# A hybrid decoder layer on one core: x requested at once over two queues, and B's keys and values as plain 512-column products behind the first products on h

## The chip, the core and the metric

The kernel runs on one core of a Trainium2 chip. The metric is the time of one execution in device microseconds; three runs of the kernel before took 1562.09, 1558.93 and 1561.91 us. The core's engines work side by side, each through its own instructions in order: TensorE (PE) multiplies, VectorE (DVE), ScalarE (ACT) and GpSimd (POOL) do the rest, SyncE (SP) mostly starts transfers. ScalarE and GpSimd can start transfers too, and every engine that does has a queue of its own for them.

## The reference

One layer on x (512 rows of 2048 numbers) with a memory of 256 rows. One projection of h = RMSNorm(x) feeds three attention branches:

```python
h = rmsnorm(x, norm_g[l])
(a_q, a_ckv, i_q, i_k, i_w, a_gate,
 b_q, b_k, b_v, b_gate,
 c_q, c_gate, mix_gate) = split_cols(h @ w_in[l], IN_SIZES)
ckv = rmsnorm(a_ckv, kv_norm_g[l])
a_k, a_v = jnp.split(ckv @ w_kv_up[l], 2, axis=-1)
...
kb = rmsnorm(b_k.reshape(bsz, seq, B_KV_HEADS, B_HEAD_DIM), k_norm_b[l])
vb = b_v.reshape(bsz, seq, B_KV_HEADS, B_HEAD_DIM)
...
m_k, m_v = jnp.split(rmsnorm(mem, mem_norm_g[l]) @ w_mem_kv[l], 2, axis=-1)
...
merged = g_a * (oa @ w_up_a[l]) + g_b * (ob @ w_up_b[l]) + g_c * (oc @ w_up_c[l])
x = x + merged @ w_o[l]
```

A attends to the 128 keys per row that an indexer (i_q, i_k, i_w) picks, B to a window of 128 rows with two key and value heads of 64 each, C to the memory. `b_k` and `b_v`, the subject here, are together 256 columns of the projection.

## The kernel before, in words

All arrays lie transposed: 128 channels on the partitions, the 512 rows of x along the free axis. A product in float32 is made of three in a shorter form: every operand is split into a high and a low part, and high x high, low x high and high x low are added up (`mm3`, L294 to L296). The high part of a weight is a cast on ScalarE (L276, `wh`), the low part a subtraction on VectorE (L278, `wl`), each for half a unit of 128 x 1024 weights (`split`).

Every half unit is one step of a fixed order. `next_hb` (L287) opens step i: it splits the half unit four steps ahead (`LA`), and then does what `plan` has put down for step i: start a transfer, square a tile of x, sum it, norm it. So the place of an instruction in its engine's queue comes from the step numbers. Raw weights have three buffers (`raw`), `wh` and `wl` six each.

The stages up to the point that matters are these.

- Memory units: 12 of the 16 units of the memory's keys and values (`mem`, L460), 6 products `mm3` of 512 columns in two half steps per unit and accumulator group. Beside them x is loaded (L368, on ScalarE's queue, three steps ahead of its use), squared (L374) and summed up (L377). The rows' mean (L379) and the inverse root (L306, GpSimd) give h through `x_norm`, `x_high` and `x_low`.
- g1 (L473): 192 products of 336 columns on h: the indexer's key and weights, and the latent a_ckv.
- The last four memory units (L589). Beside them two generators run, a step of each at every `pump()`: `g_lat` norms, scales and transposes the latent (L499 to L519), `g_comb` (L552) makes from h the sums and differences that the pairs below need, and overwrites half of h's high and low parts with one of them.
- KV (L691): the latent times `w_kv_up`, three groups of 24 products; `kv_group` (L655) squares, norms, transposes (L681) and stores keys and values. It has three buffers `sq`, some of which are held until a store (L667, L687) has landed.
- Pairs (`pair`, L780): all other projections of h go by two at a time, as a scheme of 7 products of half size (256 columns, 8 x 3 each) in the place of 8. Sums of weight tiles for it are made by GpSimd (L212) and by transfers that add (L218). `STREAM` (L96) is the order of the pairs: first B's keys and values (`bkv`), then a pair of the merge gates (`mix`), four pairs of the indexer's queries (`iq`), and so on. `kv_b` (L1040) norms and transposes B's keys after their pair.

From the indexer pairs on nothing is changed.

Of the kernel before, what the change touches and what calls it, by code (L numbers as in the profile page):

```python
# [45 lines left out]

LG = {"c0": 1, "c1": 2, "c2": 3, "c3": 1, "a0": 3, "a1": 1, "a2": 3, "a3": 3, "b0": 2, "b1": 1, "b2": 2, "b3": 2, "b4": 2, "kb0": 6, "kb1": 4, "kb2": 2, "kb3": 3, "kv0": 1, "kv1": 2, "kv2": 1, "kv3": 1, "m0": 6, "m1": 4, "m2": 3, "m3": 4, "m4": 7, "m5": 3, "l0": 2, "l1": 2, "l2": 2, "l3": 2, "iq": 1, "limit": 3, "gapc": 5, "gapa": 6, "gapb": 6, "cb0": 1, "cb1": 1, "ol": 3, "s1": 9, "s2": 5, "s3": 5, "s4": 2, "nq0a": 3, "nq1a": 1, "pta": 1, "nq0b": 3, "nq1b": 1, "ptb": 1, "nq0c": 3, "nq1c": 1, "ptc": 1}


class Pump:
# [43 lines left out]
def _stream():  # L96

    mix = [("mix", j, d) for d in range(0, KT, 2) for j in range(3)]
    s = [("bkv",), mix.pop(0)] + [("iq", j) for j in range(4)] + [mix.pop(0)]
    for name, n in (("c", HC), ("a", HA), ("b", 6)):  # L100
        for h in range(n):
            s += [(name, h), mix.pop(0)]
        if name != "b":
            s.append(mix.pop(0))
    return s + mix


STREAM = _stream()


@with_exitstack
def hybrid_layer(ctx: ExitStack, tc: tile.TileContext, xT, memT, memR, w_g1, w_un, w_up, params, consts, rel1, onehot, out):
# [139 lines left out]
    un = [w_un[k] for k in range(w_un.shape[0])]  # L252
    singles("mem", un[:K1])
    singles("g1", [w_g1[k] for k in range(8)])
    singles("mem2", un[K1:16])
    singles("kv", un[16:19])
    n_h = 19 + 4 * len(STREAM)
    pairs("h", un[19:n_h], POS["kv", 0] + 2)
    singles("upc", un[n_h:n_h + 8])
    singles("upa", [w_up[k] for k in range(16)])  # L260
    singles("upb", [w_up[k] for k in range(16, 32)])
# [102 lines left out]
            hx_new(k, F32)  # L364
        return hxf[k % 8][:, 2 * (k // 8):2 * (k // 8) + 2, :]

    def x_dma(k):
        act.dma_start(xf(k), xT[k].rearrange("p (a b) -> p a b", a=2))  # L368

    sqs = {}  # L370

# [47 lines left out]

    KO = [k + 8 * j for k in range(8) for j in range(2)]  # L420
    for k in range(KT):
        plan(k - 3, lambda k=k: x_dma(k))
        plan(k, lambda k=k: x_sq(k))
        if k:
            plan(k + 1, lambda k=k: x_sum(k))
    plan(KT + 1, rms_sum)
    plan(KT + 2, rms_pow)
    plan(KT + 4, rms_rows)
# [4 lines left out]
        plan(i_g1 - 3 + n, lambda k=k: x_norm(k))  # L433
    for c in range(8):
        i = POS["mem", 2 * c] if 2 * c < K1 else POS["mem2", 2 * c - K1]
        plan(i - 8, lambda c=c: m_dma(c))
        plan(i - 3, lambda c=c: m_split(c))


# [5 lines left out]
    dve.memset(gk, 0.0)  # L445
    act.activation(gk, gk, AF.Exp)
    sync.dma_start(pc, params)
    for f in at.pop(-8):
        f()
    tiles_["mem", 0] = wp.tile([128, 1024], F32, tag="raw", bufs=3, name=nm("wraw"))  # L450
    for c in (0, 512):
        sync.dma_start(tiles_["mem", 0][:, c:c + 512], un[0][:, c:c + 512])
    for i in range(-8, 0):
        step(i)
    plan(2, lambda: sync.dma_start(cc, consts))


# [94 lines left out]
    def g_comb():  # L552

        F = {}

        def sums(k):
            F[k] = f = cb.tile([128, 4, 256], F32, tag="tf", bufs=2, name=nm("tf"))
            b11, b12, b21, b22 = (xf(k + 8 * j)[:, c, :] for j in range(2) for c in range(2))
            dve.tensor_tensor(out=f[:, 3, :], in0=b11, in1=b12, op=ALU.subtract)
            dve.tensor_tensor(out=f[:, 0, :], in0=b22, in1=f[:, 3, :], op=ALU.add)  # L560
            dve.tensor_tensor(out=f[:, 1, :], in0=b12, in1=b22, op=ALU.subtract)
            dve.tensor_tensor(out=f[:, 2, :], in0=b21, in1=f[:, 0, :], op=ALU.subtract)

        def high(k):
            act.copy(hth[:, k, 256:], F[k][:, 3, :])
            hx_new(k, F32R)
            act.copy(hxt[k][:, 0:3, :], F[k][:, 0:3, :])

        def low(k):
            f = F.pop(k)  # L570
            dve.tensor_tensor(out=htl[:, k, 256:], in0=f[:, 3, :], in1=hth[:, k, 256:].bitcast(F32), op=ALU.subtract)
            dve.tensor_tensor(out=hxt[k][:, 3:6, :], in0=f[:, 0:3, :], in1=hxt[k][:, 0:3, :].bitcast(F32), op=ALU.subtract)

        for k in range(10):
            if 0 <= k - 2:
# [12 lines left out]


    mem(range(K1, KT))  # L590
# [578 lines left out]
        return tl("t2")  # L1169

    last = max(i for i, x in enumerate(STREAM) if x[0] == "b") + 3
    for n, item in enumerate(STREAM):
        kind = item[0]
        if n == last:
            flush()
            pump.drain()
            ws["stack"].close()
            ws.clear()
            switch("fp", {"t2": 4, "og": 1, "m": 2, "f": 1, "oxh": 1, "oxl": 1})
            oxh, oxl = tl("oxh", (128, 6, T), F32R), tl("oxl", (128, 6, T), F32R)  # L1180
            ox = [(oxh[:, k, :], oxl[:, k, :]) for k in range(6)]
            pump.back(o_load("c", ox[:4]))
        if item[0] not in ("mix", "iq") and item[-1] in ("bkv", 0):
            flush()
        if item == ("iq", 0):
            flush()
            pump.drain()
            ck_s.close()
            switch("iq", {"t2": 4, "stk": 6, "rl": 2, "mr": 2})
            pump.back(g_mem())  # L1190
            pump.back(g_index())
            pump.back(g_ik())
            pump.back(g_rel())
        elif item == ("c", 0):
            switch("c", {**BASE, "q": 2})
        elif item == ("a", 0):
            pump.drain()
            ws["stack"].close()
            cs_s.close()
            ws.clear()  # L1200
            pump.gap = LG["gapa"]
            switch("a", {**BASE, "q": 2, "T": 2, "kv": 2})
        elif item == ("b", 0):
            pump.drain()
            ws["stack"].close()
            tk_s.close()
            ws.clear()
            switch("b", {**BASE, "q": 4, "T": 2, "kb1": 1, "kb2": 1, "vb": 1})
            pump.gap = LG["gapb"]
            pump.back(b_start())  # L1210
        if kind == "bkv":
            pair(t2, t2, kv_b)
        elif kind == "iq":
            def fin(z0, z1, item=item):
                st = [stack(z, "stk") for z in (z0, z1)]

                def ready():
                    yield from lag("iq")
                    for x in range(2):
                        j = 2 * item[1] + x  # L1220
                        iq[2 * j], iq[2 * j + 1] = st[x]
                pump.back(ready())
            pair(t2, t2, fin)
        elif kind == "mix":
            def mix_fin(z0, z1, item):
                yield
                _, j, d = item
                for x, z in enumerate((z0, z1)):
# [168 lines left out]
def _layout(x, mem, norm_g, w_in, kv_norm_g, w_kv_up, idx_k_ln_g, idx_k_ln_b, q_norm_a, k_norm_a, q_norm_b, k_norm_b,  # L1397
# [13 lines left out]
    def pairs(a, b):  # L1411
# [64 lines left out]
```

## Time and profile before

| | us |
|---|---|
| runs, median of 3 | 1561.91 |
| the profiled execution | 1568.9 |
| its span | 1567.1 |
| TensorE busy | 1494.5 (95%) |
| VectorE busy | 1211.7 (77%) |
| ScalarE busy | 792.7 (51%) |
| GpSimd busy | 587.6 (37%) |
| TensorE's waits in the first 200 us, eight longest kinds | 30.4 |

The span is the profiled execution without what lies around it. Matmuls are pipelined: the time of one row of a matmul reaches into the next, so a sequence is best read from the starts of its rows. "Idle before" names what an engine had waited for when an instruction began.

### The profile page before, as it was taken

The numbers are of one execution on the slowest core, as the hardware profiler recorded it, in microseconds if no ns is written. First come the engines' busy times: TensorE is split into PE (matmuls) and PEld (weight loads), VectorE is DVE, ScalarE is ACT, GpSimd is POOL, SyncE is SP. The second block draws the span as 40 slices with busy tenths as digits, with TensorE's granted clock in tenths as the row PEclk, the third lists the DMA queues.
The fourth block names the chain that finished last, engine by engine and source line by source line (L and its number), as shares of the span: only waits on it lengthen the run. The fifth ranks groups of instructions, "written<-read, shape, count | busy, mean of one in ns | idle before, by whom it ended". The sixth has DMA issues, their size and how long they took to land. (4 is left out here: it accounts for less than half of the span.)

```text
span 1567.1 us, 29464 instructions
## 1 busy us (share of the span) xinstructions
PE 1494.5 (95%) x11066; PEld 1420.0 (91%) x11066; DVE 1211.7 (77%) x2020; ACT 792.7 (51%) x1673; POOL 587.6 (37%) x485
## 2 busy tenths in 40 slices
PE   7978998999999999999999999999989999989998
PEld 5867997989999999999999999999979888879998
DVE  5897678899997688778777778778856576996565
ACT  5555466655555455555555555555535332444342
POOL 0013442343333344333333434333323034865543
PEclk9889999999999999999999999999999999999999
DMA  8346578445446666556556555555546765547774
GB/s 300 119 124 170 160 193 218 118 128 166 122 144 180 174 183 183 178 135 189 179 156 170 160 136 165 173 128 168 156 132 180 248 205 169 180 124 196 201 196 129
DMA packets 98792, 263.75 MB, mean 168 GB/s; under 512 B 10356, under 2 KB 23796, under 8 KB 98650
## 3 DMA queue, kind: packets, MB, share of 16 engines
q1 hardware_dynamic: 78746, 197.77, 36.4%
q0 software_dynamic: 15264, 55.58, 20.0%
q10 hardware_dynamic: 4640, 8.52, 1.8%
q8 instruction: 87, 1.43, 0.4%
q14 instruction: 55, 0.45, 0.1%
HBM read 237.12 MB, written 29.04 MB: 170 GB/s over the span
## 5 line engine op out<-in xcount | busy, mean ns | idle before, releaser
L294 PE MATMUL p<-hth,wh 128*128 128x256 f32 (+1 forms) x1792 | 532.4, 297 | 12.0 <-ACT hth L1276 5.4
L295 PE MATMUL p<-htl,wh 128*128 128x256 f32 (+1 forms) x1792 | 521.7, 291 | 2.3 <-DVE htl L1278 2.3
L296 PE MATMUL p<-hth,wl 128*128 128x256 f32 (+1 forms) x1792 | 522.1, 291 | 1.4 <-DVE wl L278 1.3
L294 PE MATMUL p<-hx,wh 128*128 128x256 f32 x1272 | 371.0, 292 | 0.8 <-DVE t L763 0.8
L294 PEld LDWEIGHTS p<-hth,wh 128*128 128x128 f32 x1792 | 347.6, 194 | 22.5 <-ACT hth L1276 5.6
L296 PE MATMUL p<-hx,wl 128*128 128x256 f32 x1272 | 361.8, 284 | 0.0
L295 PE MATMUL p<-hx,wh 128*128 128x256 f32 x1272 | 361.8, 284 | 0.0
L295 PEld LDWEIGHTS p<-htl,wh 128*128 128x128 f32 x1792 | 347.5, 194 | 9.2 <-DVE htl L1278 2.6
L296 PEld LDWEIGHTS p<-hth,wl 128*128 128x128 f32 x1792 | 347.2, 194 | 5.9 <-DVE wl L278 2.1
L278 DVE TENSOR_TENSOR wl<-wS,wh 128x512 fp32r<-128x512 f32 x318 | 277.4, 886 | 78.6 <-ACT wh L276 77.8
L278 DVE TENSOR_TENSOR wl<-wraw,wh 128x512 fp32r<-128x512 f32 (+2 forms) x346 | 262.3, 767 | 86.9 <-ACT wh L276 79.5
L212 POOL TENSOR_TENSOR wS<-wS,wA 128x512 f32<-128x512 f32 x106 | 162.4, 1553 | 420.3 <-DMA wA<-in_w_un 243.0
L276 ACT CAST wh<-wraw 128x512 fp32r<-128x512 f32 (+2 forms) x346 | 202.7, 591 | 122.6 <-PE p L295 65.9
L294 PEld LDWEIGHTS p<-hx,wh 128*128 128x128 f32 x1272 | 245.6, 193 | 5.1 <-issue 1.7
L295 PEld LDWEIGHTS p<-hx,wh 128*128 128x128 f32 x1272 | 245.7, 193 | 0.8
L278 DVE TENSOR_TENSOR wl<-wA,wh 128x512 fp32r<-128x512 f32 x212 | 182.3, 860 | 82.3 <-ACT wh L276 80.6
L296 PEld LDWEIGHTS p<-hx,wl 128*128 128x128 f32 x1272 | 245.4, 193 | 0.0
L276 ACT CAST wh<-wS 128x512 fp32r<-128x512 f32 x318 | 192.0, 617 | 102.6 <-POOL wS L212 52.7
L212 POOL TENSOR_TENSOR wS<-wraw,wS 128x512 f32<-128x512 f32 x106 | 171.0, 1649 | 18.9 <-DVE wl L278 15.1
L276 ACT CAST wh<-wA 128x512 fp32r<-128x512 f32 x212 | 125.9, 617 | 96.4 <-DMA wA<-in_w_un 55.5
L306 POOL TENSOR_TENSOR r<-rv,cc 128x4 f32<-128x4 f32 (+2 forms) x30 | 40.7, 1358 | 235.6 <-DVE rv L305 235.4
L218 POOL DMA_DIRECT2D wS<-in_w_un x53 | 58.6, 1106 | 43.9 <-DMA wS<-in_w_un 30.6
(224 smaller groups left out, 1986.7 us busy)
## 6 DMA issues: line engine op xcount, KB each, us to landing
wraw<-in_w_un SPq DMA_DIRECT2D x132, 512.0 KB, 5.7
wS<-in_w_un SPq DMA_DIRECT2D x53, 512.0 KB, 5.7
wA<-in_w_un SPq DMA_DIRECT2D x53, 512.0 KB, 3.7
wS<-in_w_un POOLq DMA_DIRECT2D x53, 512.0 KB, 7.8
wA<-in_w_un POOLq DMA_DIRECT2D x53, 512.0 KB, 5.5
th_d<-t SPq DMA_DIRECT2D x48, 256.0 KB, 4.5
t<-th_d SPq DMA_DIRECT2D x48, 256.0 KB, 3.0
wraw<-in_w_up SPq DMA_DIRECT2D x32, 384.0 KB, 3.8
```

The source lines that it names most:

```text
L212: pool_e.tensor_tensor(out=tiles_[key][:, s], in0=tiles_[a][:, s], in1=tiles_[b][:, s], op=op)
L218: pool_e.dma_start(tiles_[key], unit, accum_op=ALU.add)
L276: act.copy(h[:, :w], s)
L278: e.tensor_tensor(out=l[:, :w], in0=s, in1=h[:, :w].bitcast(F32), op=ALU.subtract)
L294: pe.matmul(o, ah, bh, start=first, stop=False, skip_group_check=True)
L295: pe.matmul(o, ah, bl, start=False, stop=False, skip_group_check=True)
L296: pe.matmul(o, al, bh, start=False, stop=last, skip_group_check=True)
L306: pool_e.tensor_tensor(out=r[:, :n], in0=v[:, :n], in1=cc[:, C_NH:C_NH + n], op=ALU.pow)
```

## The change

Two things change. The transfers of x are no longer planned three steps ahead of their use on ScalarE's queue: the eight even tiles are asked for on ScalarE's queue ahead of its first cast, the eight odd ones on SP's queue between the first weights. And B's keys and values leave the pairs: they become 96 products `mm3` of 512 columns in two accumulators (keys, values), between g1 and the last four memory units, with four weight units of their own. The combinations of tile k wait until these products have read h's tile k. Two lags of the latent's generator are cut from 2 to 1. `kv_b` is called just ahead of the stream of pairs.

```diff
-    s = [("bkv",), mix.pop(0)] + [("iq", j) for j in range(4)] + [mix.pop(0)]
+    s = [mix.pop(0)] + [("iq", j) for j in range(4)] + [mix.pop(0)]
...
     singles("g1", [w_g1[k] for k in range(8)])
+    for n in (0, 2):
+        POS["bkv", n] = i = len(split_src)
+        for m in (n, n + 1):
+            plan(i - 8 + 2 * (m - n), raw(("bkv", m), un[19 + (0, 1, 3, 2)[m]]))
+        for c in (0, 512):
+            split_src.extend(src(("bkv", m), c, c + 512) for m in (n, n + 1))
     singles("mem2", un[K1:16])
...
-        plan(k - 3, lambda k=k: x_dma(k))
...
+    for k in range(KT):
+        if k % 2 == 0:
+            x_dma(k, act)
     for i in range(-8, 0):
         step(i)
+        if i >= -6:
+            x_dma(2 * i + 13, sync)
+    x_dma(13, sync)
+    x_dma(15, sync)
...
             if 0 <= k - 1 < 8:
+                while done.get("bkv", -1) < k - 1:
+                    yield
                 high(k - 1)
...
+    kv = [psum(t, "kv") for t in ("o", "a")]
+    for n in range(8):
+        wh, wl = next_hb()
+        for k in range(4):
+            s = slice(k * 128, k * 128 + 128)
+            i = 4 * (n // 2) + k
+            mm3(kv[n % 2], wh[:, s], wl[:, s], hth[:, i, :], htl[:, i, :], i == 0, i == KT - 1)
+        if n % 2:
+            done["bkv"] = i
+        pump()
+    zkv = [tl("t2"), tl("t2")]
+    act.copy(zkv[0], kv[0])
+    dve.tensor_copy(out=zkv[1], in_=kv[1])
     mem(range(K1, KT))
...
+    kv_b(*zkv)
     for n, item in enumerate(STREAM):
...
-        if kind == "bkv":
-            pair(t2, t2, kv_b)
```

The start of SP's queue before: `mr` is a tile of the memory (two channels blocks), `wraw` a raw unit, `pc` the parameters. No tile of x is here; they stand in ScalarE's queue between its casts.

```order
L447 DMA pc<-in_params 128x102
L407 DMA mr_125<-in_memT 128x2x256
L452 DMA wraw_127<-in_w_un 128x512 x2
L196 DMA wraw_130<-in_w_un 128x1024
L196 DMA wraw_136<-in_w_un 128x1024
L407 DMA mr_138<-in_memT 128x2x256
L196 DMA wraw_156<-in_w_un 128x1024
L196 DMA wraw_174<-in_w_un 128x1024
```

The start of SP's queue in the changed kernel; `hx` are tiles of x.

```order
L413 DMA mr_125<-in_memT 128x2x256
L458 DMA wraw_127<-in_w_un 128x512 x2
L196 DMA wraw_142<-in_w_un 128x1024
L374 DMA hx_144<-in_xT 128x512
L374 DMA hx_146<-in_xT 128x512
L196 DMA wraw_152<-in_w_un 128x1024
L413 DMA mr_154<-in_memT 128x2x256
L374 DMA hx_156<-in_xT 128x512
L374 DMA hx_168<-in_xT 128x512
L196 DMA wraw_174<-in_w_un 128x1024
L374 DMA hx_144<-in_xT 128x512
L374 DMA hx_146<-in_xT 128x512
```

Two more tiles of x follow there (`hx_156`, `hx_168`) before the fifth unit, `wraw_192`. Eight tiles of x thus stand ahead of that unit in SP's queue. ScalarE's queue starts with eight more, ahead of its first cast:

```order
L453 ACTIVATE gk<-gk 128x3
L374 DMA hx_130<-in_xT 128x512
L374 DMA hx_132<-in_xT 128x512
L374 DMA hx_134<-in_xT 128x512
L374 DMA hx_136<-in_xT 128x512
L374 DMA hx_130<-in_xT 128x512
L374 DMA hx_132<-in_xT 128x512
L374 DMA hx_134<-in_xT 128x512
L374 DMA hx_136<-in_xT 128x512
L282 CAST wh_148<-wraw_127 128x512
```

Before, the first of them stood behind two casts. VectorE's order up to the last sum of squares is the same in both kernels but for the names.

VectorE behind g1, before, from the latent's sum of squares (`ss`) to the latent's scaling (`Wk`): `wl` is the low part of a half memory unit, `tf` a combination of a tile of h, `hx` and `htl` its low parts.

```order
L492 TENSOR_REDUCE ss_940<-sq_895 128x2
L492 TENSOR_REDUCE ss_940<-sq_896 128x2
L305 TENSOR_SCALAR rv_943<-ss_940 128x4
L278 TENSOR_TENSOR wl_948<-wraw_855,wh_947 128x512
L571 TENSOR_TENSOR htl<-tf_899,hth 128x256
L572 TENSOR_TENSOR hx_917<-tf_899,hx_917 128x768
L559 TENSOR_TENSOR tf_964<-hx_164 128x256
L560 TENSOR_TENSOR tf_964<-hx_164,tf_964 128x256
L561 TENSOR_TENSOR tf_964<-hx_164 128x256
L562 TENSOR_TENSOR tf_964<-hx_164,tf_964 128x256
L278 TENSOR_TENSOR wl_970<-wraw_855,wh_969 128x512
L509 TENSOR_TENSOR Wk<-Wk,r_944 128x4x256
```

The same place in the changed kernel; these `wl` belong to B's key and value units.

```order
L284 TENSOR_TENSOR wl_897<-wraw_806,wh_896 128x512
L505 TENSOR_REDUCE ss_916<-sq_885 128x2
L505 TENSOR_REDUCE ss_916<-sq_886 128x2
L311 TENSOR_SCALAR rv_919<-ss_916 128x4
L284 TENSOR_TENSOR wl_924<-wraw_845,wh_923 128x512
L522 TENSOR_TENSOR Wk<-Wk,r_920 128x4x256
L572 TENSOR_TENSOR tf_943<-hx_144 128x256
L573 TENSOR_TENSOR tf_943<-hx_144,tf_943 128x256
```

The scaling of the latent (L509, now L522) stands behind one combination of a tile (four rows) where it stood behind three, and TensorE's products in its shadow are those on h.

## Rows read from the trace of the kernel before

**Rows 1.** TensorE's waits, 0 to 200 us: total us, times, longest.

```profile
PE mb L294 <- ACT mh L416: 7.5, 4, 2.7
PE p L681 <- DVE t L677: 5.0, 2, 3.1
PE p L514 <- DVE Wk L509: 4.2, 1, 4.2
PE pk L294 <- ACT ckh L517: 3.3, 1, 3.3
...
PE p L681 <- ACT sq L684: 2.9, 1, 2.9
PE p L299 <- DVE t L377: 2.8, 1, 2.8
```

**Rows 2.** TensorE's timeline: start, us, engine, line, out<-in, idle before.

```profile
43.73 1.87 PE L299 MATMUL p<-cc,t 128*128 128x1 f32 x8 [2.81 <-DVE t L377]
...
58.12 0.31 PE L294 MATMUL g<-wh,hth 128*128 128x336 f32 x1
...
87.56 0.39 PE L294 MATMUL mb<-wh,mh 128*128 128x512 f32 x1
...
95.53 0.39 PE L296 MATMUL mb<-wh,ml 128*128 128x512 f32 x1
...
108.92 0.80 PE L294 MATMUL pk<-wh,ckh 128*128 128x512 f32 x1 [3.34 <-ACT ckh L517]
...
139.13 0.56 PE L294 MATMUL p<-hth,wh 128*128 128x256 f32 x1
...
161.98 0.28 PE L294 MATMUL p<-hth,wh 128*128 128x256 f32 x1
```

**Rows 3.** Stretches: us, busy time of each engine, granted clock, DMA share, GB/s.

```profile
10.00:40.00 30.00, 25.12 (x100) 18.85 (x99) 21.27 (x38) 19.55 (x38) 0.00 (x0) 0.96 0.92 322
43.70:58.10 14.40, 14.37 (x58) 12.13 (x59) 7.49 (x15) 5.16 (x11) 1.04 (x1) 0.78 0.30 91
88.00:125.00 37.00, 26.79 (x103) 20.49 (x101) 36.26 (x76) 22.34 (x43) 4.18 (x3) 0.86 0.42 118
```

**Rows 4.** Waits of all engines, 0 to 160 us.

```profile
ACT sq L374 <- DMA hx<-in_xT: 9.1, 6, 3.2
```

**Rows 5.** Transfers, 0 to 60 us in 40 slices of 1.5 us.

```profile
GB/s 0 90 292 354 381 295 199 272 340 221 397 396 305 363 283 366 369 281 292 358 328 284 397 395 308 269 324 79 70 160 211 18 0 29 201 0 29 201 116 113
```

**Rows 6.** VectorE's timeline beside the memory units.

```profile
18.30 0.69 DVE L278 TENSOR_TENSOR wl<-wraw,wh 128x512 fp32r<-128x512 f32 x1
...
20.72 0.68 DVE L278 TENSOR_TENSOR wl<-wraw,wh 128x512 fp32r<-128x512 f32 x1
...
24.52 0.88 DVE L417 SCALAR_TENSOR_TENSOR ml<-mr,pc,mh 128x256 fp32r<-128x256 f32 x2
...
43.00 0.68 DVE L377 TENSOR_TENSOR t<-t,sq 128x512 f32<-128x512 f32 x1
```

**Rows 7.** VectorE's timeline, first and last row of the combinations.

```profile
88.56 0.42 DVE L559 TENSOR_TENSOR tf<-hx 128x256 f32<-128x256 f32 x1
...
124.15 0.95 DVE L572 TENSOR_TENSOR hx<-tf,hx 128x768 fp32r<-128x768 f32 x1
```

**Rows 8.** Timeline of SP, GpSimd and ScalarE in KV.

```profile
105.61 0.33 SPq L196 DMA_DIRECT2D wS<-in_w_un  x1
...
109.56 1.06 POOL L218 DMA_DIRECT2D wS<-in_w_un  x1 [13.12 <-ACT ckh L517]
...
115.25 1.72 POOL L212 TENSOR_TENSOR wS<-wS,wA 128x512 f32<-128x512 f32 x1 [4.62 <-DMA wS<-in_w_un]
...
129.08 1.30 POOL L212 TENSOR_TENSOR wS<-wS,wA 128x512 f32<-128x512 f32 x1
...
130.93 0.59 ACT L662 ACTIVATE sq<-pk 128x512 f32<-128x512 f32 x1
...
137.98 0.47 ACT L684 ACTIVATE sq<-p,gk 128x256 f32<-128x256 f32 x1 [3.31 <-DMA kv_d<-sq]
```

More of the change, by code (lines that the diff above doesn't have):

```diff
@@ L45 @@
 B_PERM = [h for i in range(6) for h in (i, 6 + i)]
-LG = {"c0": 1, "c1": 2, "c2": 3, "c3": 1, "a0": 3, "a1": 1, "a2": 3, "a3": 3, "b0": 2, "b1": 1, "b2": 2, "b3": 2, "b4": 2, "kb0": 6, "kb1": 4, "kb2": 2, "kb3": 3, "kv0": 1, "kv1": 2, "kv2": 1, "kv3": 1, "m0": 6, "m1": 4, "m2": 3, "m3": 4, "m4": 7, "m5": 3, "l0": 2, "l1": 2, "l2": 2, "l3": 2, "iq": 1, "limit": 3, "gapc": 5, "gapa": 6, "gapb": 6, "cb0": 1, "cb1": 1, "ol": 3, "s1": 9, "s2": 5, "s3": 5, "s4": 2, "nq0a": 3, "nq1a": 1, "pta": 1, "nq0b": 3, "nq1b": 1, "ptb": 1, "nq0c": 3, "nq1c": 1, "ptc": 1}
+LG = {"c0": 1, "c1": 2, "c2": 3, "c3": 1, "a0": 3, "a1": 1, "a2": 3, "a3": 3, "b0": 2, "b1": 1, "b2": 2, "b3": 2, "b4": 2, "kb0": 6, "kb1": 4, "kb2": 2, "kb3": 3, "kv0": 1, "kv1": 2, "kv2": 1, "kv3": 1, "m0": 6, "m1": 4, "m2": 3, "m3": 4, "m4": 7, "m5": 3, "l0": 1, "l1": 1, "l2": 2, "l3": 2, "iq": 1, "limit": 3, "gapc": 5, "gapa": 6, "gapb": 6, "cb0": 1, "cb1": 1, "ol": 3, "s1": 9, "s2": 5, "s3": 5, "s4": 2, "nq0a": 3, "nq1a": 1, "pta": 1, "nq0b": 3, "nq1b": 1, "ptb": 1, "nq0c": 3, "nq1c": 1, "ptc": 1}
 class Pump:
@@ L254, in hybrid_layer @@
     singles("g1", [w_g1[k] for k in range(8)])
+    for n in (0, 2):
[4 more added lines that the diff above has]
+            split_src.extend(src(("bkv", m), c, c + 512) for m in (n, n + 1))
     singles("mem2", un[K1:16])
     singles("kv", un[16:19])
-    n_h = 19 + 4 * len(STREAM)
-    pairs("h", un[19:n_h], POS["kv", 0] + 2)
+    n_h = 23 + 4 * len(STREAM)
+    pairs("h", un[23:n_h], POS["kv", 0] + 2)
     singles("upc", un[n_h:n_h + 8])
@@ L365, in xf, with x_dma @@
         return hxf[k % 8][:, 2 * (k // 8):2 * (k // 8) + 2, :]
-    def x_dma(k):
-        act.dma_start(xf(k), xT[k].rearrange("p (a b) -> p a b", a=2))
+    def x_dma(k, q):
+        q.dma_start(xf(k), xT[k].rearrange("p (a b) -> p a b", a=2))
     sqs = {}
@@ L421, in hybrid_layer @@
     for k in range(KT):
-        plan(k - 3, lambda k=k: x_dma(k))
-        plan(k, lambda k=k: x_sq(k))
+        i = k
+        plan(i, lambda k=k: x_sq(k))
         if k:
-            plan(k + 1, lambda k=k: x_sum(k))
+            plan(i + 1, lambda k=k: x_sum(k))
     plan(KT + 1, rms_sum)
@@ L435, in hybrid_layer @@
         i = POS["mem", 2 * c] if 2 * c < K1 else POS["mem2", 2 * c - K1]
-        plan(i - 8, lambda c=c: m_dma(c))
+        if c:
+            plan(i - 8, lambda c=c: m_dma(c))
         plan(i - 3, lambda c=c: m_split(c))
@@ L447, in hybrid_layer @@
     sync.dma_start(pc, params)
-    for f in at.pop(-8):
-        f()
+    m_dma(0)
     tiles_["mem", 0] = wp.tile([128, 1024], F32, tag="raw", bufs=3, name=nm("wraw"))
@@ L1182, in hybrid_layer @@
             pump.back(o_load("c", ox[:4]))
-        if item[0] not in ("mix", "iq") and item[-1] in ("bkv", 0):
+        if item[0] not in ("mix", "iq") and item[-1] == 0:
             flush()
@@ L1210, in hybrid_layer @@
             pump.back(b_start())
-        if kind == "bkv":
-            pair(t2, t2, kv_b)
-        elif kind == "iq":
+        if kind == "iq":
             def fin(z0, z1, item=item):
@@ L1427, in _layout @@
              np.ascontiguousarray(w_kv_up[0].reshape(2, 128, 3, 512).transpose(2, 1, 0, 3)[::-1]).reshape(3, 128, 1024)]
+    units.append(P["bkv"].reshape(4, 128, 1024))
     for it in STREAM:
```

## The prediction

> **What bounds the kernel now.** I read the page's busy lines first: TensorE works for 95% of the span, so the change can only give back TensorE's idle or slow time, or change its work. The waits of TensorE over the first 200 us [rows 1] come next. They lie where the change is: 7.5 us on the memory tile `mh` in the opening stage, 2.8 us on the sum of squares of x (L377), and, after the products on h for the indexer ("g1"), 4.2 us on the latent's scaling (L509), 3.3 us on `ckh`, 5.0 and 2.9 us on the key transposes (L681). The third view, TensorE's timeline, gives the stages [rows 2]: the row sum at 43.73, g1 from 58.12, the last four memory units from 87.56, the up-projection of the latent ("KV") from 108.92, B's key/value pair from 139.13, the first `mix` pair from 161.98. Everything behind 161.98 should only slide, so the change is worth the shift of that first mix product.
>
> Two stretches differ in what is late. Up to 40 us it is the transfers: the DMA engines are busy for 92% at 322 GB/s [rows 3], and ScalarE waits 9.1 us for tiles of x [rows 4]. From 88 to 125 it is VectorE, busy 36.26 of 37.0 us, with TensorE at 26.79 [rows 3].
>
> **Part 1: x asked for at once.** Removed: ScalarE's waits for x. Not removed: one byte, and not one row of VectorE's order changes in this stage. What moves is who is served first. In the new order of SP's queue eight tiles of x stand ahead of the fifth memory unit, and ScalarE's queue asks for the other eight before its first cast. Ahead of and including unit 4 there are then (counted from the two orders, KB) parameters 51, two memory tiles 512, five units 2560, 16 tiles of x 4096: 7219 KB = 7.39 MB. At 322 GB/s that is 22.9 us, from 3 us on, since little moves before [rows 5]: 25.9; with a cast before it VectorE splits unit 4 at about 27.0. Before, that split ran at 20.72 [rows 6]. So the weights come 6 us later.
>
> From that split to the last sum of squares VectorE has 13 splits, 13 sums and 3 pairs of memory splits. From 18.30 to 20.72 it starts four of the first two kinds, 0.605 us each; a pair takes 0.88 [rows 6]: 26 x 0.605 + 3 x 0.88 = 18.4 us, without a wait now, as x is there. The last sum ends at 27.0 + 18.4 = 45.4, against 43.00 + 0.68 = 43.7. What late weights cost, the removed waits nearly return. Behind the sum stand 14.4 us until g1 (43.73 to 58.12), run at a granted clock of 0.78 [rows 2, 3] after the 2.8 us wait. At 1.366 us a half unit (six products of 0.228, from 35 rows between 87.56 and 95.53) the seven half units need 9.6, the 16 small products 1.9 at full clock: 11.5. In the new order TensorE starts unit 4 near 29 and has nine half units (12.3) and a slow start before the row sum, so it arrives near 43 and waits about 2: I take 12.0. G1 starts at 57.4: **-0.7 us**. Bounds: with unit 4 no later than before, 20.72 + 18.4 + 12 = 51.1, -7.0; at 250 GB/s 6.7 us later and at the low clock, +8.4.
>
> On the rate the Trainium skill ("DMA: Bandwidth & Descriptors", section on where 436 GB/s comes from) says that loads from HBM are bound at about 358 GB/s per core. The slices here reach 397 [rows 5], so as a cap the rule does not hold; as an average it would be an estimate above the 322 measured. By it the 7.39 MB take 20.6 us and this term is about -3.0 instead of -0.7.
>
> **Part 2: keys and values of B as plain products behind g1.** Removed: a pair of 7 x 24 = 168 products of 256 columns, 22.85 us from 139.13 to 161.98 with the last key transposes inside. Added: 8 steps of 12 = 96 products of 512 columns, 96 x 0.228 = 21.9 us. TensorE's work is about equal; the place is not. New chain from 87.56: 21.9 + eight transposes 1.0 + the four memory units 48 x 0.228 = 10.9, so 121.4 if nothing waits. The latent's scaling now has four steps (10.9 us) of cover before its transposes, so the 4.2 and 3.3 go.
>
> VectorE does not get less to do. Its combinations for the pairs run from 88.56 to 124.15 + 0.95 = 125.1 [rows 7], 36.5 us. In the new order there stand between the same two rows two more splits (1.2), one more memory pair (0.9) and one bank copy less (0.6, taken like a split): 38.0, ending at 126.6; the second split that KV's first product needs stands 1.3 ahead, 125.3. So KV starts at about 125, and TensorE waits some 3.8 us for VectorE in small pieces. KV itself took 30.2 us before (108.92 to 139.13) for 72 x 0.228 = 16.4 of products and some 2.4 of transposes. Its waits had two sources. Combinations still in ScalarE's and VectorE's queues: these are over now. The other stays: the weights of the first pair. The first tile is asked for when the memory units are done (105.61), added to at 109.56, summed from 115.25 to 116.97, 11.4 us after the asking; GpSimd's four roots (0.7 each) and the second half of the sum (1.30) follow, and ScalarE, which casts that half, squares the next group at 130.93, 8.2 us before the pair; 3.31 of these it waits for a store of keys [rows 8]. New: memory units done at 124, sum at 135.4, second half at 139.5, squares at 140.5, pair 4.9 to 8.2 later; I take 147.3, since the store's wait may shrink but not go. Now that is the mix pair: 147.3 against 161.98 is **-14.7 us**. Bounds: KV at its products alone, 125 + 18.8 = 143.8, -18.2; KV as long as before, 155.2, -6.8.
>
> **Small terms.** The wait added to the combinations (until the products have read h) is covered: they are late by VectorE alone, and TensorE's readings are done 10 us earlier. B's key norm starts at the same place of the mix pair as before. There are 14 half steps less between KV and the drain ahead of the indexer pairs: nothing, at worst another 2.9 like the last wait of rows 1; I put +0.3.
>
> **Sum.** -0.7 - 14.7 + 0.3 = -15.1 us. The profiled execution took 1568.9 (span 1567.1), 7.0 above the median; the terms are differences, so 1561.9 - 15.1 = **1547**.
>
> **Rivals.** A (the forecast): part 2 gives 15, part 1 nothing.
> B: the early x is a gain too, since the second queue does not hold back the weights. For it: ScalarE's 9.1 us of waits and slices near 400. Against: 92% busy engines already with both queues. G1 at 51.1 instead of 57.4: 1540.5.
> C: KV keeps its length, as its tail hangs on weights, roots and stores rather than on the combinations. For it: the last wait, 2.9, is of this kind. Against: 5.0 of the waits end with VectorE. -6.8 for -14.7: 1554.7.
> D, slower: x in front starves the weights. Place: units 2 to 4. For it: a slice at 199 GB/s where both queues first run [rows 5]. Price: at 180 GB/s unit 4 is split at 45, the sum ends at 63.5, and with the low clock (14.4) g1 starts at 77.9, +19.8; with part 2 at -14.4 that is 1567. It eats the whole gain below some 207 GB/s. Against: the mean of 322.
>
> **How the numbers follow.** A 0.60, B 0.10, C 0.21, D 0.09. From A's own 1541 to 1553, with the lower half of C's and B's sides: 1538 to 1557 for 8 in 10. No change means within 0.2% (3.1 us), about what a measurement of this kernel can tell. Faster: A, B and most of C (0.60 + 0.10 + 0.17); within: the rest of C and some of D (0.04 + 0.02); slower: 0.07.
>
> **What would show it.** Right, if TensorE's wait on L509 is gone and its first KV product comes 36 to 39 us behind g1's end, if VectorE is busy over 95% in between, if g1 starts at 55 to 60, and if TensorE's waits on `mh` now stand before 30 us, with none on the row sum above 2.8. Part 1 is wrong if g1 starts before 54 or after 62, part 2 if the first mix product comes less than 55 or more than 66 us behind g1's end (74.4 before).

## The result, and the profile after

The changed kernel takes 1551.12 us (median of six runs, 1549.86 to 1557.65) against 1562.00 (six runs, 1558.93 to 1570.67): ratio 0.9932, 95% interval 0.9911 to 0.9953, that is 10.9 us less (7.3 to 13.9). The forecast was 1547, a gain of 15.1: it came out 4 us smaller. The profiled execution took 1549.86, its span is 1548.1, 19.0 under that of before: more than the medians differ by, and what to make of that is a question below.

TensorE's waits over the first 200 us (us in total, times, longest), which answer to [rows 1]:

```profile
PE mb L300 <- ACT mh L422: 6.8, 1, 6.8
PE p L711 <- DVE t L707: 3.4, 2, 2.9
PE p L305 <- DVE t L383: 2.5, 1, 2.5
...
PE mb L301 <- DVE wl L284: 2.2, 2, 1.7
...
PE p L711 <- ACT sq L714: 1.3, 1, 1.3
```

The scaling of the latent (4.2) and `ckh` (3.3) are gone from the list. The memory tile `mh` has one wait in place of four, of nearly the same length: it has moved to the very start. Of KV's end 4.7 of 7.9 us are left.

TensorE's timeline, the marks of [rows 2] (start, us, instruction, idle before), with one more at the bottom, the pair behind the first `mix` pair:

```profile
13.26 0.79 PE L300 MATMUL mb<-wh,mh 128*128 128x512 f32 x1 [6.81 <-ACT mh L422]
...
42.13 1.05 PE L305 MATMUL p<-cc,t 128*128 128x1 f32 x8 [2.55 <-DVE t L383]
...
55.18 0.31 PE L300 MATMUL g<-wh,hth 128*128 128x336 f32 x1
...
84.62 0.39 PE L300 MATMUL kv<-hth,wh 128*128 128x512 f32 x1
...
120.97 0.39 PE L300 MATMUL pk<-wh,ckh 128*128 128x512 f32 x1
...
145.93 0.36 PE L300 MATMUL p<-hth,wh 128*128 128x256 f32 x1
...
168.68 0.36 PE L300 MATMUL p<-hth,wh 128*128 128x256 f32 x1
```

g1 starts 2.9 us earlier, KV stands 36.35 us behind g1's end (84.62), and the first `mix` pair at 145.93 instead of 161.98. The same pair begins at these marks in both kernels, but it is not the same work that lies before them; the last mark shows that below.

The stretches that answer to [rows 3] (us, busy time of PE, PEld, DVE, ACT and POOL, granted clock, DMA share, GB/s):

```profile
10.00:20.00 10.00, 6.74 (x17) 5.20 (x18) 5.55 (x11) 6.60 (x14) 0.00 (x0) 0.53 1.05 390
10.00:40.00 30.00, 26.32 (x102) 21.06 (x102) 24.02 (x43) 24.42 (x49) 0.00 (x0) 0.84 0.87 316
23.95:42.07 18.12, 15.63 (x69) 12.60 (x68) 18.12 (x33) 17.02 (x34) 0.00 (x0) 1.00 0.70 240
42.10:55.20 13.10, 13.07 (x59) 10.94 (x60) 7.47 (x15) 4.87 (x10) 1.04 (x1) 0.87 0.32 102
85.00:122.00 37.00, 34.82 (x156) 27.93 (x154) 35.58 (x78) 22.62 (x43) 1.39 (x1) 1.00 0.29 102
```

From 85 to 122 VectorE is as full as from 88 to 125 before (35.58 of 37.0), but TensorE now has 34.82 us of work beside it instead of 26.79, at full clock instead of 0.86: that is part 2. From 10 to 20 the transfers run at 390 GB/s, while over 10 to 40 their mean is 316, no more than the 322 of before.

ScalarE's and SP's requests and first casts, and VectorE's rows that answer to [rows 6]:

```profile
2.38 9.24 ACTq L374 DMA_DIRECT2D hx<-in_xT  x6
11.66 1.14 ACT L282 CAST wh<-wraw 128x512 fp32r<-128x512 f32 x2 [9.41 <-DMA hx<-in_xT]
...
3.12 3.68 SPq L374 DMA_DIRECT2D hx<-in_xT  x2
...
14.33 2.69 SPq L374 DMA_DIRECT2D hx<-in_xT  x4
17.59 0.33 SPq L196 DMA_DIRECT2D wraw<-in_w_un  x1
...
23.95 0.69 DVE L284 TENSOR_TENSOR wl<-wraw,wh 128x512 fp32r<-128x512 f32 x1 [1.53 <-ACT wh L282]
...
41.37 0.70 DVE L383 TENSOR_TENSOR t<-t,sq 128x512 f32<-128x512 f32 x1
```

Six requests took ScalarE 9.24 us, and its first cast had to wait behind them until 11.66. Before, it stood at 5.31:

```profile
5.31 0.62 ACT L276 CAST wh<-wraw 128x512 fp32r<-128x512 f32 x1 [3.07 <-DMA wraw<-in_w_un]
```

SP was held up in the same way and asked for unit 4 only at 17.59. VectorE splits unit 4 at 23.95 and ends the last sum at 42.07, 18.1 us later, with no gap.

### The profile page after: what moved, and what is told of

It reads as the page before. It is cut to its first block, busy times and chain, and to the rows that moved or that the text cites. A ratio compares the mean times of both kernels' runs of the same rounds, so it can differ in the third digit from the quotient of the medians.

```text
span 1548.1 us, 29281 instructions
## 1 busy us (share of the span) xinstructions
PE 1488.6 (96%) x10994; PEld 1413.0 (91%) x10994; DVE 1205.2 (78%) x2011; ACT 787.5 (51%) x1665; POOL 574.2 (37%) x478
## 5 line engine op out<-in xcount | busy, mean ns | idle before, releaser
L300 PE MATMUL p<-hth,wh 128*128 128x256 f32 (+1 forms) x1760 | 521.7, 296 | 7.9 <-DVE t L1361 5.4
L302 PE MATMUL p<-hth,wl 128*128 128x256 f32 (+1 forms) x1760 | 511.4, 291 | 1.3 <-DVE wl L284 1.3
L301 PE MATMUL p<-htl,wh 128*128 128x256 f32 (+1 forms) x1760 | 511.2, 290 | 0.7 <-DVE htl L1307 0.7
L300 PE MATMUL p<-hx,wh 128*128 128x256 f32 x1248 | 362.5, 290 | 1.7 <-DVE t L793 1.5
L300 PEld LDWEIGHTS p<-hth,wh 128*128 128x128 f32 x1760 | 340.5, 193 | 18.3 <-ACT hx L1305 5.7
L302 PE MATMUL p<-hx,wl 128*128 128x256 f32 x1248 | 353.9, 284 | 0.0
L301 PE MATMUL p<-hx,wh 128*128 128x256 f32 x1248 | 353.7, 283 | 0.0
L284 DVE TENSOR_TENSOR wl<-wraw,wh 128x512 fp32r<-128x512 f32 (+2 forms) x350 | 275.0, 795 | 87.6 <-ACT wh L282 85.9
L284 DVE TENSOR_TENSOR wl<-wS,wh 128x512 fp32r<-128x512 f32 x312 | 261.2, 851 | 78.6 <-ACT wh L282 78.4
L212 POOL TENSOR_TENSOR wS<-wS,wA 128x512 f32<-128x512 f32 x104 | 154.6, 1506 | 405.1 <-DMA wA<-in_w_un 221.6
L300 PEld LDWEIGHTS p<-hx,wh 128*128 128x128 f32 x1248 | 239.7, 192 | 5.8 <-ACT wh L282 2.3
L301 PEld LDWEIGHTS p<-hx,wh 128*128 128x128 f32 x1248 | 239.9, 192 | 0.7
L212 POOL TENSOR_TENSOR wS<-wraw,wS 128x512 f32<-128x512 f32 x104 | 167.0, 1639 | 18.9 <-DVE wl L284 15.1
```

The costliest lines, as they stand in the source:

```text
L212: pool_e.tensor_tensor(out=tiles_[key][:, s], in0=tiles_[a][:, s], in1=tiles_[b][:, s], op=op)
L284: e.tensor_tensor(out=l[:, :w], in0=s, in1=h[:, :w].bitcast(F32), op=ALU.subtract)
L300: pe.matmul(o, ah, bh, start=first, stop=False, skip_group_check=True)
L301: pe.matmul(o, ah, bl, start=False, stop=False, skip_group_check=True)
L302: pe.matmul(o, al, bh, start=False, stop=last, skip_group_check=True)
```

## The experiments

All ratios are to the kernel before in runs on the same chip. What the profiles of the first comparison show, in start times; "next" is the pair behind the first `mix` pair, "rest" the time from there to the end of the span:

| profiled execution | row sum | g1 | KV | mix | next | rest |
|---|---|---|---|---|---|---|
| before | 43.73 | 58.12 | 108.92 | 161.98 | 183.37 | 1383.7 |
| before_again | 43.96 | 57.04 | 107.84 | 159.90 | 181.28 | 1383.6 |
| before_third | 43.23 | 57.90 | 108.70 | 158.85 | 180.23 | 1381.1 |
| x_only | 42.02 | 56.70 | 107.50 | 158.03 | 179.41 | 1380.7 |
| kv_only | 41.05 | 55.87 | 121.66 | 146.28 | 170.17 | 1385.0 |
| after | 42.13 | 55.18 | 120.97 | 145.93 | 168.68 | 1379.4 |
| after_again | 42.12 | 55.22 | 121.01 | 145.58 | 168.33 | 1383.9 |
| pad15 | 41.91 | 54.98 | 120.77 | 159.35 | 182.37 | 1383.2 |

**The early x alone (x_only).** Against the kernel before:

```diff
-        plan(k - 3, lambda k=k: x_dma(k))
...
+    for k in range(KT):
+        if k % 2 == 0:
+            x_dma(k, act)
     for i in range(-8, 0):
         step(i)
+        if i >= -6:
+            x_dma(2 * i + 13, sync)
+    x_dma(13, sync)
+    x_dma(15, sync)
...
```

> Part 1 alone: all of x asked for at once over two queues, the keys and values of B still the first pair on h. Theory (the parts add up as in the two traces): the last sum of squares ends near 42.1 instead of 43.7, g1 starts near 55.2 instead of 58.1, nothing behind it changes its length, KV's first product comes 51 us after g1's start as before, the total is 2.9 us shorter: 1559 against 1562, ratio 0.998. Rival (the early x is given back, which would explain why the medians differ by 10.9 us where the first mix product moved by 16): g1 starts near 55 but the total is within 1 us of before or longer, ratio 1.000 to 1.003.

Measured: 1564.54 against 1564.56 (12 and 24 runs), ratio 1.0006 (0.9992 to 1.0020). The theory's 0.998 lies outside this interval, the rival's 1.000 to 1.003 begins inside it: the total shows no gain, between 1.3 us gained and 3.1 lost. The row sum comes 1.2 to 1.9 us earlier than in the three profiles of before (42.02, as the theory said), but g1 only 0.3 to 1.4 (56.70, not 55.2), as the way from the row sum to g1 took 14.7 us. KV stands 50.8 us behind g1 as in those. Behind that nothing is lengthened (rest 1380.7), so the trace has no place where the early x is given back later; a microsecond of an early g1 can't be told from the spread of the opening.

**B's keys and values alone (kv_only).** Against the changed kernel:

```diff
+        plan(k - 3, lambda k=k: x_dma(k))
...
-    for k in range(KT):
-        if k % 2 == 0:
-            x_dma(k, act)
     for i in range(-8, 0):
         step(i)
-        if i >= -6:
-            x_dma(2 * i + 13, sync)
...
```

> Part 2 alone: the keys and values of B as plain products behind g1, x asked for step by step as before. Theory: g1 starts at 58.1 as before, KV's first product comes 36 to 37 us behind g1's end, the first mix product 61 to 62 us behind it, 13.1 us earlier than before; the total is 13 us shorter, 1549, ratio 0.9916. Rival (part 2 is worth only what the medians leave it, 10.9 less 2.9): 8 us, ratio 0.995. Second rival (the end of KV hangs on the store of keys and on the weights, and not on what is before it): KV takes 30 us as before and the total is 6 to 7 us shorter, ratio 0.9955.

Measured: 1554.66, ratio 0.9946 (0.9928 to 0.9963), 8.4 us less (5.8 to 11.3). The theory's 13 us (0.9916) are outside; the first rival's 8 us are what the runs gave. KV takes 24.6 us, not 30, so the second rival falls by its mechanism, though its 6 to 7 us lie inside the interval. From g1's start to "next" there are 114.3 us, against 122.3 to 125.3 in the four executions with B's pair. KV stands 36.35 us behind g1's end, the first `mix` pair 61.0. Unforeseen: g1 at 55.87 and the row sum at 41.05, although this opening is that of before. One execution cannot say whether that is chance.

**Both kernels again (before_again, before_third, after_again).** No edit.

> The kernel before once more, for its profile. If the 7 us that its profiled execution lay above the median come from the stages ahead of the first mix product, this one has that product at 155 to 158 with 1405 us behind it; if they come from behind it, the product is at 162 again and 1397 to 1400 us follow. The stages ahead of it should agree within 0.5 us if they are fixed by the order and not by chance.

> The kernel before a third time, for its stages. Theory (the two profiles of before lay high by chance behind the first mix product): KV's first product 50.8 us behind g1's, B's pair 28.9 to 30.3 us behind that, and an execution near the median of 1564 has 1400 to 1403 us behind the first mix product. Rival: it has 1405 again, and the medians differ from the profiles because of the stages ahead: the mix product then stands at 157 or earlier.

> The changed kernel once more. Theory: ratio 0.993 again (0.991 to 0.995), g1 at 55 us, the first mix product at 146, about 1402 behind it. Rival: the low time of the first profile was luck ahead of the mix product, and it stands at 149 to 151 here.

Measured: 1566.70, 1563.08, and 1553.93 with ratio 0.9940 (0.9919 to 0.9961), 9.4 us less. I had expected the stages ahead of the `mix` pair to agree within 0.5 us, and they do not: in the three executions of before it stands at 161.98, 159.90 and 158.85. In before_again 1405.0 us follow it, so its time lies ahead of the mark and behind it, in neither place alone. In before_third 1402.5 follow, as the theory said, and its KV and B's pair are the shortest of the three. In the changed kernel the pair came at 145.58, so its first profile was no luck ahead of that mark; but 1406.6 us follow, where I had expected 1402. B's pair alone took 22.85, 23.06 and 21.53. Two executions of before, the first from the forecast's own trace (columns as above):

```profile
139.13:161.98 22.85, 22.85 (x182) 22.85 (x181) 15.91 (x22) 12.52 (x23) 11.76 (x11) 0.93 0.74 204
161.98:183.37 21.39, 21.39 (x183) 21.39 (x181) 14.59 (x23) 10.46 (x19) 8.29 (x7) 1.00 0.52 140
```

```profile
137.32:158.85 21.53, 21.53 (x184) 21.53 (x183) 17.13 (x22) 12.87 (x24) 11.42 (x11) 1.00 0.74 212
158.85:180.23 21.38, 21.38 (x183) 21.38 (x181) 15.36 (x23) 10.47 (x19) 8.91 (x7) 1.00 0.54 144
```

The pair that the change takes out costs 21.5 us at full clock. In the forecast's execution it began in a stretch at the low clock behind TensorE's last wait (2.9 us), mean 0.93, and I took that for its length. But in the other execution the low clock lay more in KV, just ahead of the pair (0.82 instead of 0.90):

```profile
108.92:139.13 30.21, 20.93 (x85) 15.82 (x85) 25.61 (x52) 16.34 (x35) 10.78 (x11) 0.90 0.57 140
```

```profile
108.70:137.32 28.62, 22.57 (x85) 17.07 (x85) 25.49 (x51) 15.83 (x34) 10.21 (x11) 0.82 0.62 160
```

KV and B's pair together hold 43.8, 43.8, 44.1 and 44.1 us of TensorE's busy time in before, before_again, before_third and x_only. What makes the forecast's execution longer than before_third from KV on is TensorE's idle time in KV: 9.3, 8.3, 6.1 and 6.5 us, in the same order.

The first `mix` pair takes 21.4 in all four executions with B's pair in front of it, and 22.75 in both of the changed kernel:

```profile
145.93:168.68 22.75, 22.75 (x195) 22.75 (x193) 15.85 (x26) 13.39 (x26) 11.98 (x9) 1.00 0.68 197
```

That is 1.37 us more, with TensorE never idle and the clock full: it holds more instructions (195 records for 183). TensorE's timeline says which, the key transposes of KV's last groups, first of the changed kernel, then of before:

```profile
145.51 0.66 PE L711 MATMUL p<-cc,t 128*128 128x128 f32 x4 [1.32 <-ACT sq L714]
147.44 0.60 PE L711 MATMUL p<-cc,t 128*128 128x128 f32 x4
149.31 0.60 PE L711 MATMUL p<-cc,t 128*128 128x128 f32 x4
151.19 0.60 PE L711 MATMUL p<-cc,t 128*128 128x128 f32 x4
```

```profile
141.83 0.74 PE L681 MATMUL p<-cc,t 128*128 128x128 f32 x4
143.84 0.60 PE L681 MATMUL p<-cc,t 128*128 128x128 f32 x4
145.71 0.60 PE L681 MATMUL p<-cc,t 128*128 128x128 f32 x4
```

Three groups stood inside B's pair. With that pair gone they stand inside the `mix` pair, behind the mark by which I counted the gain. "Next" is a mark behind everything that moved; there the shift is 168.5 against 181.6 (mean of two, of three), 13.1 us.

**The rest only slides (pad15).**

```diff
-            for k in range(2):
-                mm3(p, ckh[:, k, t], ckl[:, k, t], hbs[k][0], hbs[k][1], k == 0, k == 1)
+            for _ in range(12 if (n, i) == (2, 3) else 1):
+                for k in range(2):
+                    mm3(p, ckh[:, k, t], ckl[:, k, t], hbs[k][0], hbs[k][1], k == 0, k == 1)
```

> The changed kernel with the last group of KV's products done twelve times instead of once (66 further products of 512 columns, 0.228 us each: 15.0 us), so that everything from the first mix product on starts 15.0 us later, about where it started before the change. Theory (what lies behind the first mix product only slides): 15.0 us above the changed kernel, ratio 1.003 to before. Rival (some of a shift at this place is taken back behind it, which is why the medians gained 10 where the first mix product moved by 15): only 9 to 11 us above the changed kernel, ratio 1.000.

Measured: 1567.24, ratio 1.0017 (1.0004 to 1.0031), 12.7 us above the changed kernel's mean ratio of 0.9936. At "next" it is 13.9 later (182.37 against 168.5): of the 15.0 added the 1.3 us wait ahead of the pair is covered. The rest is 1383.2. The theory's 1.003 lies inside the interval, the rival's 1.000 just outside. The 12.7 themselves lie between the theory's 15.0 and the rival's 9 to 11, and with the intervals of both ratios they are known to about 3 us; the trace decides it. Over all 14 profiles the rest is 1382.3 on average with B's pair in the stream (four, 1380.7 to 1383.7) and 1382.7 without it (ten, 1379.4 to 1385.0). So nothing is seen to be taken back behind the change; the scatter of the 14 leaves about 2 us either way (an estimate from their spread). One execution differs from another by up to 5.6 us in this rest alone, which is why two profiles with spans 19.0 us apart prove nothing about the last 5.

**ScalarE's requests between its casts (ask_late).**

```diff
-    for k in range(KT):
-        if k % 2 == 0:
-            x_dma(k, act)
     for i in range(-8, 0):
         step(i)
+        x_dma(2 * i + 16, act)
```

> ScalarE's eight requests for x go out one after each step of the opening, between its first casts, and not all ahead of the first one. Theory (the row sum is set by the arrival of the fifth memory unit at about 23.2 us and VectorE's 18.1 us behind it): the first memory product stands at 8 to 10 us instead of 13.2, the row sum between 41 and 42.2, g1 between 54 and 55.5, and no time is gained. Rival (ScalarE's stall until 11.6 us is what holds the stage): the row sum moves forward by the same 4 us, to 38, and g1 to 51.

Measured (one execution, 1554.75): first memory product at 9.15, row sum at 41.83, g1 at 54.93, as the theory says. ScalarE's stall of 9.24 us costs nothing:

```profile
6.18 0.62 ACT L282 CAST wh<-wraw 128x512 fp32r<-128x512 f32 x1 [3.94 <-DMA wraw<-in_w_un]
...
13.88 0.62 ACT L282 CAST wh<-wraw 128x512 fp32r<-128x512 f32 x1 [2.02 <-DMA hx<-in_xT]
```

The casts start 5.5 us earlier and wait for transfers soon after. SP's queue is not changed by this edit: unit 4 is asked for at 16.98 behind SP's last four tiles of x, and split at 23.65 (17.59 and 23.95 in the changed kernel). What SP's stall costs no run shows.

**A third of the sums on GpSimd (sums_pool).**

```diff
+        if k % 3 == 0:
+            pool_e.tensor_tensor(out=accp, in0=accp, in1=sqs.pop(k), op=ALU.add)
+        else:
...
+        if k == KT - 1:
+            dve.tensor_tensor(out=accx, in0=accx, in1=accp, op=ALU.add)
```

> Every third addition to the sum of squares goes to GpSimd with an accumulator of its own, and VectorE adds the two at the end: VectorE has 5 additions less and 1 more. Theory (VectorE is the limit up to the row sum): 4 x 0.605 = 2.4 us less, the row sum at 39.7, where TensorE arrives without a wait, g1 at 52.8. Rival (VectorE gets slower where GpSimd works beside it): its operations take longer than 0.605 us in this stage and the row sum stays at 41.5 or later.

Measured (one execution, 1555.69): row sum at 44.67, g1 at 58.36: the rival, and later still than the 41.5 that it named. GpSimd's and VectorE's timelines:

```profile
21.54 1.35 POOL L386 TENSOR_TENSOR t<-t,sq 128x512 f32<-128x512 f32 x1 [20.27 <-ACT sq L382]
...
40.14 3.76 POOL L386 TENSOR_TENSOR t<-t,sq 128x512 f32<-128x512 f32 x1 [2.93 <-ACT sq L382]
...
21.66 1.78 DVE L388 TENSOR_TENSOR t<-t,sq 128x512 f32<-128x512 f32 x1
...
43.92 0.69 DVE L390 TENSOR_TENSOR t<-t,t 128x512 f32<-128x512 f32 x1 [1.16 <-POOL t L386]
```

GpSimd takes 1.35 to 3.76 us for an addition that takes VectorE 0.69. Beside four of its five additions VectorE lost 1.0 to 1.1 us (1.78 instead of 0.69 in the row shown), beside the fifth GpSimd took the 3.76, and VectorE waited 1.16 for it. The Trainium skill ("Perfetto Trace Analysis", the section on optimizing scalar and DVE operations) warns that these two engines share a read port to SBUF and that moving work between them may not help; these rows agree that it did not help, and that the two delay each other; that the port is the reason they do not show. My theory that VectorE alone sets the row sum was too simple as well: in the changed kernel ScalarE works 17.02 of the same 18.12 us, so unloading VectorE could have given an estimated one microsecond at most.

**KV's tail (roots_first, sq4, two_roots_sq4).** `roots_first` puts GpSimd's first half sum of the first pair's weights behind all four roots of the second column group; `sq4` has a fourth buffer for squares and stores; the third has that buffer and the sum behind two roots, with (1, 1) for (1, 3). `own[0]` is that half sum, which the plan had put down ahead of the roots. Against the changed kernel:

```diff
             pump.back(kv_group(n, i, p))
             pump()
+            if (n, i) == (1, 3):
+                own[0]()
...
-    switch("p1", {"rb": 1, "t2": 5, "sq": 3})
+    switch("p1", {"rb": 1, "t2": 5, "sq": 4})
```

> GpSimd's first half sum of the first pair's weights is issued behind the four roots of KV's second column group, and not ahead of them. Theory (the chain weights, sum, root, key transposes is what is left of KV's waits, the mechanism of rival C): TensorE's wait of 2.5 to 2.9 us on the scaled keys is gone, the first mix product stands at 142.5 to 143.5 instead of 145.6 to 145.9. Rival (stores and the second half sum hold the end of KV anyway): the wait moves to the later transposes and the mix product stays at 145 or later.

> Only the fourth buffer for squares and stores. Theory (stores hold ScalarE, 6.5 us in four waits between KV's first product and the first pair): its waits for stores fall below 3 us and the pair's first product comes 23.3 us behind KV's first product instead of 24.6 to 25.0. Rival: the 2.5 to 2.9 us wait on the scaled keys, set by GpSimd's order, stays and the distance changes by less than 0.5 us.

> The changed kernel with two edits in KV's tail: GpSimd's first half sum of the first pair stands behind the first two roots of the second column group (not ahead of all four, and not behind all four), and ScalarE has four buffers for squares and stores instead of three. Theory (two things hold KV's end, the order root behind sum on GpSimd, and the store that frees ScalarE's buffer): the waits of 2.5 to 2.9 us on the scaled keys and of 1.3 us before the first pair go, the first pair's first product stands 21 to 22.5 us behind KV's first product instead of 24.6 to 25.0, the total 2 to 4 us below the changed kernel, ratio 0.991 to 0.992 to before. Rival (the weights' own chain, asked for at 121, holds the end): the distance stays at 24 or more and the ratio at 0.993 to 0.995.

Measured, from KV's first product to the pair's: 24.6 to 25.0 in the changed kernel, 26.2 with `roots_first` (one execution, 1555.68), 23.1 with `sq4` (one execution, 1550.83), 22.1 with `two_roots_sq4`. To "next" it is 47.3 to 47.7, 49.3, 46.0 and 46.9. TensorE's waits on the keys in `roots_first`, then in `two_roots_sq4`:

```profile
133.80 0.44 PE L716 MATMUL p<-cc,t 128*128 128x128 f32 x2 [0.35 <-DVE t L712]
136.37 0.44 PE L716 MATMUL p<-cc,t 128*128 128x128 f32 x2 [0.73 <-DVE t L712]
142.97 0.41 PE L716 MATMUL p<-cc,t 128*128 128x128 f32 x2 [4.76 <-DVE t L712]
```

```profile
135.07 0.44 PE L716 MATMUL p<-cc,t 128*128 128x128 f32 x2 [1.04 <-DVE t L712]
139.49 0.41 PE L716 MATMUL p<-cc,t 128*128 128x128 f32 x2 [2.59 <-DVE t L712]
146.25 0.66 PE L716 MATMUL p<-cc,t 128*128 128x128 f32 x4 [1.48 <-ACT sq L719]
```

With all roots first the sum is late, the split of the pair's weights stands ahead of the third scaling on VectorE, and the wait moves there: the rival.

With the fourth buffer alone ScalarE's waits for stores fall from 6.6 to 3.0 us and the pair comes as early as the theory said, while the wait on the scaled keys stays (2.81), as the rival said. Most of this gain is still there at "next" (1.3 to 1.7 us).

With both edits KV is 2.7 us shorter, inside the theory's 21 to 22.5, but the waits that were to go have not gone: 1.04 and 2.59 on the scaled keys, and 1.48 moved into the `mix` pair, 5.1 us in all against 4.7 in the changed kernel. KV is shorter as the last of them stands behind the mark and as TensorE ran it at a granted clock of 1.00 instead of 0.93 (first the changed kernel, then both edits):

```profile
120.97:145.93 24.96, 20.21 (x86) 15.38 (x84) 15.85 (x34) 12.89 (x29) 10.24 (x11) 0.93 0.79 218
```

```profile
121.00:143.09 22.09, 18.38 (x86) 14.29 (x84) 16.52 (x34) 12.37 (x27) 9.53 (x11) 1.00 0.88 238
```

The `mix` pair then takes 24.76 us, and "next" stands at 167.85 instead of 168.5. The total is 1553.19, ratio 0.9919 (0.9895 to 0.9943), which can't be told from the changed kernel's 0.9932 and 0.9940. By the mark at the `mix` pair it was a gain of 2.7, by the mark behind it of 0.7.

**The lags of the latent (lags).**

```diff
-"l0": 1, "l1": 1
+"l0": 2, "l1": 2
```

> The two lags of the latent's scaling back at 2 steps, as before the change, the rest as changed. Theory (the eight new steps give cover enough): no wait on the scaling, on its transposes or on the latent's tiles; KV's first product 65.7 to 65.9 us behind g1's first one, as in the changed kernel. Rival: the latent is late again and TensorE waits 1 to 3 us for it.

Measured (one execution, 1555.45): no wait on the scaling, its transposes or the latent's tiles. KV's first product stands 64.79 us behind g1's first, 1.0 less than in the changed kernel, and "next" at 170.68, 2.2 more, with a wait of 2.58 us ahead of B's key transposes. The theory is right on the waits, though not on KV's place (65.7 to 65.9); what the lags are worth in all, one execution doesn't say.

## Why the prediction was right, and where 4 us went

**Right.** The change gains where part 2 was said to work. KV's first product stands 36.35 us behind g1's end (forecast 37.4), VectorE is busy for 96% from 85 to 122, the waits on the scaling and on `ckh` are gone, g1 starts at 55.2 (in the 55 to 60), the waits on `mh` stand before 30 us, none on the row sum is above 2.8. Part 2 alone gives 8.4 us, of 10.9 and 9.4 for the whole change. Rival D, weights starved by x, had its stall but not its price: the transfers ran at 390 GB/s where it decided under 207.

**Part 1, the term -0.7.** Net it holds: alone it makes the time 0.9 us longer (1.3 gained to 3.1 lost), and the changed kernel and kv_only differ by 0.9 of 9.4. Three steps inside were off. The 322 GB/s were a mean over 10 to 40 us, with slices down to 221; from 10 to 20, with x asked for at once, the rate was 390, and unit 4 was split at 23.95, not 27.0. Taken from the first fast slices of [rows 5] the term would have been larger. By the 358 GB/s that the Trainium skill gives as a core's bound for loads from HBM ("DMA: Bandwidth & Descriptors", the section on where 436 GB/s comes from) the split would have come at an estimated 24.7 (3 + 20.6 + the 1.1 of the forecast); as an average it was the nearer figure, and as a cap the 390 over 10 us speak against it. Then I counted a request as free: eight of them held ScalarE until 11.66, and eight SP's request for unit 4 until 17.59, 5.7 us ahead of its first cast. ScalarE's part made TensorE's start late (13.26) and at the low clock (0.53 from 10 to 20), and still cost nothing (ask_late); SP's part stands in the 23.95. Last, behind the row sum I took 12.0 us: it took 13.1 in both executions of the changed kernel, and 14.7 in x_only.

**Part 2, the term -14.7: mis-sized.** The `mix` pair stands where the forecast had it (145.93 against 147.3 - 0.7 = 146.6), and that is the trap: two errors cancel there. g1 came 2.2 us earlier than forecast, and counted from g1's end the pair came 61.3 us behind instead of 59.7. It was KV: it began 36.35 us behind g1's end, 1.1 less than forecast, but took 25.0 us (24.6 in the second execution) instead of 22.3. That is 1.6 us of the term. On the chain that I took for it, the first half sum of the pair's weights ended 12.9 us after they were asked for (121.16 to 134.09), where I took over the 11.4 of before. Two more pieces come from the mark and from the trace:

- "Removed: ... 22.85 us from 139.13 to 161.98 with the last key transposes inside": the transposes are not removed but moved behind the mark, 1.4 us.
- From g1's start to "next" the forecast's own execution took 125.25 us. With the other three that have B's pair (124.24, 122.33, 122.71) the mean is 123.6: it was 1.6 us long, by TensorE's idle time in KV.

Without these three the term is 10.1. The traces have 123.6 against 113.6, the mean of both executions of the changed kernel and of kv_only: 10.0. kv_only's runs gave 8.4 (5.8 to 11.3). So the mechanism was right, and about a third of the size did not come.

**The small term, +0.3.** The wait at the drain ahead of the indexer pairs, where I feared up to 2.9 us, is 2.4 and 2.5 us in the changed kernel and 2.9 to 3.2 in the three executions of before: nothing was added.

**Rival C** had its mechanism, but not its size: KV kept 24.6 to 25.0 of its 28.6 to 30.2 us, and the waits left are those it named (roots behind the sum on GpSimd, the store's buffer). A fourth buffer takes some 1.5 us of them away in one execution; the waits on the roots no edit took away.

**Open.** At "next" both parts together give 13.1 us in the traces, which is inside the first comparison's interval (7.3 to 13.9) and 0.4 outside the second's (6.1 to 12.7). 10.6 of them lie between g1 and "next", as much as the medians have in all (10.9 and 9.4). The other 2.5 lie ahead of g1 (57.7 on average in three executions of before, 55.2 in two of the changed kernel), and the runs do not show them: x_only's gain nothing. Much of it may be which executions were profiled: the three of before lay 6.9 and 2.1 us above and 2.3 below the medians of the runs beside them, 2.3 above on average. And the opening of before is not fixed by its order: kv_only, with the same opening, had its row sum at 41.05 and g1 at 55.87, and moved 344 and 355 GB/s from 10 to 20 and from 20 to 30 us, where the three executions of before moved 289 to 338. Why is not known; more profiles of before would be needed.

## What to carry to other kernels

Measure a shift at a mark behind everything that the edit can push across it: a stage that ends early with its last work slid into the next one has gained less than its mark says. Count a stage from the end of the one before it: an early start can hide that it has become longer. Before a stage is booked as removed, look at the granted clock that its duration was measured at, at a second execution, and at the stage ahead of it, where the low clock may lie in that other execution. A mean rate over a stretch is not the rate while much is outstanding; take the slices.

## What the runs showed of the hardware that was not expected

- Requests for transfers are not free to the engine that issues them: in the changed kernel six of 256 KB took ScalarE's queue 9.24 us, four on SP 2.69, and ScalarE's cast behind them waited until 11.66. Spread between the casts (ask_late), two took 2.26 us and the later ones 0.33 to 0.36 each.
- A GpSimd addition of 128x512 took 1.35 to 3.76 us beside a busy VectorE, and an addition of VectorE beside it 1.78 instead of 0.68 (sums_pool).
- From the row sum to g1, the same work took 13.1 us in seven of the fourteen profiles and 13.7 to 14.8 in the others; 14.40 us at a granted clock of 0.78 before, 13.10 at 0.87 after, behind waits of TensorE of about the same length (2.8 and 2.5 us).
- TensorE's low clock can fall into either of two neighbouring stages with the sum unchanged: KV and B's pair ran at granted clocks of 0.90 and 0.93 in the forecast's execution and of 0.82 and 1.00 in before_third, with 43.8 and 44.1 us of busy time in the two together.
